# Half strips of the convolution's taps through two buffers, their read-back on the queue of the weights, and three small reorderings at the joints of a four-layer trunk

## The chip, the core and the metric

The kernel runs on one core of a Trainium2 chip. A core has five engines with queues of their own: PE (matrix products; PEld in the profile is its weight load), DVE and ACT (elementwise work), POOL (elementwise work and, here, issuing of some transfers) and SP (which here only issues transfers). Each engine works through its own instructions in the order in which they stand, and waits where another engine or a transfer has not delivered yet. The metric is the device time of one execution in microseconds, the median of the runs; lower is better.

## What is computed

A trunk of four layers over 256 frames of width 1024. Layers 0 and 3 mix the frames by retention, layer 1 by a Conformer convolution, layer 2 by stick-breaking attention, and each layer ends with an MLP with a squared ReLU. The parts of the reference that matter here:

```python
for i in range(DEPTH):                       # DEPTH = 4, kinds 0, 1, 2, 0
    h = rms_norm(x, norm_mix[i])
    m = (retention_mixer, conformer_conv_mixer, stick_breaking_mixer)[i % 3](h, ...)
    x = x + m
    x = x + squared_relu_mlp(rms_norm(x, norm_ffn[i]), ffn_w1[i], ffn_w2[i])   # width 4096
return rms_norm(x, final_norm)

def rms_norm(x, w):
    return x * lax.rsqrt(jnp.mean(x * x, axis=-1, keepdims=True) + EPS) * w

def conformer_conv_mixer(xn, pw1_w, pw1_b, dw_w, dw_b, ln_w, ln_b, pw2_w, pw2_b):
    h = xn @ pw1_w + pw1_b
    a, gate = jnp.split(h, 2, axis=-1)
    h = a * jax.nn.sigmoid(gate)
    h = lax.conv_general_dilated(h, dw_w[:, None, :], (1,), [(30, 0)], ..., feature_group_count=1024) + dw_b
    return jax.nn.silu(layer_norm(h, ln_w, ln_b)) @ pw2_w + pw2_b
```

All weights and the output are float32, and every matrix product is made of three products of rounded parts (high x high, high x low, low x high).

## The kernel before

**Weights.** The weights of all layers are one stream of units of 128x1024 numbers, in the order of a table (PLAN). Two units are one chunk of 1 MB, which SP fetches into a tile `raw` (L348, three buffers). `unit_hi` casts a unit to its high part `wh` on ACT (L360), `unit_lo` takes the rest `wl` on DVE (L367); the pool holds five such pairs. PE then multiplies: `mm_w` (L571 low, L575 high) in the first product of the MLP, `triple` (L687) in its second product, `mm_b` (L555 to L557) in the first product of the convolution. A cast is issued where the program fetches the unit, and stands in ACT's queue at that place.

**Norms.** The sum of squares of x, which the norm ahead of each mixer and MLP needs, is collected by `norm_sq`: a square on ACT (L485) for each of the four tiles of x, and an addition (L490) on POOL or on DVE. `norm_r` turns the sum into a factor through PE (L435) and DVE; `bcast` (L442, L448) spreads a factor over the partitions through PE and ACT into the tile `rb`. The products of a mixer are started on x without the factor; it is multiplied in later. At the joint of two layers `middle` leaves the last part of x to be finished inside the first product of the next mixer, and leaves the last two squares to `norm_late`, which the mixer calls.

In the MLP of a retention layer, ACT's relu (L633) and square (L635) take the output of the first product, after ACT (L599) and DVE (L600) have put its halves together. ACT's buffers for that come from the pool `t2` (tiles `t`), of ten.

**Strips.** Six of the convolution's eight groups of channels are done on PE as products with small diagonal matrices. Those matrices, 18 strips of 128x512, are made in layer 0 by `make_strips`: for each of the 36 halves POOL multiplies a pattern by the taps into a tile `st` (L881), and then POOL issues a transfer of `st` to a strip in the chip's main memory (L885). `st` has one buffer. At the start of the convolution POOL issues 18 transfers that read the strips back into tiles of the pool `big` (L1112, 256 KB each, 36 buffers).

```python
o = self.bc.tile([P, S], F32, name=self.nm("st"), tag="lnb", bufs=1)
nc.gpsimd.tensor_mul(...)                              # L881
nc.gpsimd.dma_start(d[:, e * S : (e + 1) * S], o)      # L885
```

**MLP's second product.** `down` walks over the 16 blocks of rows, first those in MIXED (some by Strassen's scheme from sums of raw weights, L383 to L391 on DVE and ACT), then REST, first the left 512 columns, then the right. The places at which `middle` scales a finished part (L761 on ACT), turns it (L774 on PE) and adds it to x (L781 on DVE) are set by `hook`.

**Order.** PE and DVE keep the order of the program where the code says so (`keep_in_program_order`, `manual_schedule`); elsewhere a scheduler places an instruction, and `issue_after(ins)` forbids it to stand ahead of `ins`.

Of the kernel before, what the change touches and what calls it, by code (L numbers as in the profile page):

```python
# [8 lines left out]
F32 = mybir.dt.float32  # L9
# [6 lines left out]
P = 128  # L16
D = 1024
S = 256
# [224 lines left out]
class Trunk:  # L243
    def __init__(self, ctx, tc, xT, w, prm, cst, fin, gn, out):
        self.tc, self.nc = tc, tc.nc
        self.w_d, self.out_d, self.x_d, self.fin_d, self.gn_d = w, out, xT, fin, gn
        pool = lambda name, bufs, **k: ctx.enter_context(tc.tile_pool(name=name, bufs=bufs, **k))
        self.cp = pool("cp", 1)
        self.raw = pool("raw", 3)
        self.wp = pool("wp", 5)  # L250
        self.zp = pool("zp", 1)
        self.big = pool("big", 36)
        self.t2 = pool("t2", 10)
        self.colp = pool("colp", 3)
        self.bc = pool("bc", 2)
        self.prp = pool("prp", 3)
        self.dram = pool("dram", 2, space=bass.MemoryType.DRAM)
        self.acc_p = pool("acc", 4, space=bass.MemoryType.PSUM)
        self.mis_p = pool("mis", 4, space=bass.MemoryType.PSUM)
        self.n = 0  # L260
        self.un = 0
        self.rest = self.end = None
        self.sums = []
        nc = self.nc
        head = self.cp.tile([P, NP0 + 512], F32, name="head", tag="head")
        self.prm0 = head[:, :NP0]
        self.x = [head[:, NP0:]]
        self.prm = self.cp.tile([P, NPCOL - NP0], F32, name="prm", tag="prm")
        self.cst = self.cp.tile([P, NCCOL], F32, name="cst", tag="cst")
        self.first = [self.raw.tile([P, RAWW], F32, name=f"raw{n}", tag="raw") for n in range(3)]  # L270
        self.ones = self.tmp().bitcast(mybir.dt.bfloat16)[:, :512]
        nc.gpsimd.memset(self.ones, 1.0)
        self.warm(11)

        def weights(n, a, b, queue=nc.sync):
# [60 lines left out]
    def unit_hi(self, key):  # L336
        nc = self.nc
        assert PLAN[self.un] == key, (PLAN[self.un], key)
        o = self.un % UPC
        if o == 0:  # L340
            n = self.un // UPC
            if n < len(self.first):
                self.rawt = self.first[n]
            else:
                self.rawt = self.raw.tile([P, RAWW], F32, name=self.nm("raw"), tag="raw")
                h = 1024 if n < 4 else UPC * 1024
                for a in range(0, UPC * 1024, h):
                    nc.sync.dma_start(self.rawt[:, a : a + h], self.w_d[n][:, a : a + h])  # L348
            i = self.un // UPC - DST
            if 0 <= i < RH:  # L350
                n = CCOL["D"] + i * 384
                self.tc.keep_in_program_order(nc.sync.dma_start(self.cst[:, n : n + 384], self.cst_d[:, n : n + 384]))
        o = self.un % UPC
        src = self.rawt[:, o * 1024 : (o + 1) * 1024]
        hi = self.wp.tile([P, 1024], F32R, name=self.nm("wh"), tag="wh")
        lo = self.wp.tile([P, 1024], F32R, name=self.nm("wl"), tag="wl")
        n = 512 if self.un < 2 * UPC else 1024
        cuts = [slice(i, i + n) for i in range(0, 1024, n)]
        for s in cuts:
            nc.scalar.copy(hi[:, s], src[:, s])  # L360
        self.un += 1
        return hi, lo, src, cuts
# [119 lines left out]
    def norm_sq(self, p, engine=None):  # L482
        nc = self.nc
        q = self.tmp()
        nc.scalar.activation(out=q, in_=self.x[p], func=AF.Square)  # L485
        if self.sq is None:
            self.sq = q
        else:
            a = self.tmp()
            (engine or nc.gpsimd).tensor_add(a, self.sq, q)  # L490
            self.sq = a
# [16 lines left out]


    def norm_late(self):  # L510
        if self.sums:
            with self.tc.issue_after(self.z_ins):
                self.norm_sq(self.sums.pop(0), self.nc.vector)

# [167 lines left out]
    def down(self, i, h, fast, begin, hook):  # L682
# [49 lines left out]
        nc.vector.tensor_add(uq, u, e5)  # L732
        nc.vector.tensor_add(C[1, 1], C[1, 1], uq)

        for c in range(2):
            w, late = {}, REST[-2] if c else REST[-1] + 1
            steps = [(kb, kk, t) for kb in REST if kb < late for kk in range(2) for t in range(2)]
            steps += [(kb, kk, t) for t in range(2) for kb in REST if kb >= late for kk in range(2)]
            for kb, kk, t in steps:
                if kb not in w:  # L740
                    w[kb] = plain(kb, c)
                if c:
                    hook(C, (kb, kk, t))
# [125 lines left out]
    def make_strips(self):  # L869
# [6 lines left out]
        for i in range(len(PET)):  # L876
            for v in vs:
                d = self.dram.tile([P, 512], F32, name=self.nm("strip"), tag=f"strip{len(self.strips)}", bufs=1)
                for e in range(2):
                    o = self.bc.tile([P, S], F32, name=self.nm("st"), tag="lnb", bufs=1)  # L880
                    nc.gpsimd.tensor_mul(  # L881
                        v3(o, 8, 32), self.c("id32", 32).unsqueeze(1).to_broadcast([P, 8, 32]),
                        v[:, i * 16 + e * 8 : i * 16 + e * 8 + 8].unsqueeze(2).to_broadcast([P, 8, 32]),
# [5 lines left out]
    def retention(self, j, nxt):  # L889
# [6 lines left out]
        for h in range(RH):  # L896
            for isk in range(2):
# [4 lines left out]
                else:  # L902
                    with self.tc.issue_after(self.z_ins) if j and not h and isk else nullcontext():
                        args = "ret_w_in", j, isk * D + h * DK, self.zs
                        ps = self.pair_w(*args, keep=h == isk == 0) if j else self.pair_b(*args)
                    for _ in range(2):
                        self.norm_late()
                sq = self.tmp()
                nc.scalar.activation(out=sq, in_=ps, func=AF.Square)
                g = self.tmp()  # L910
# [189 lines left out]
    def conv(self, j, nxt):  # L1100
# [3 lines left out]
        rb = None  # L1104


        strip, h4, hs4 = {}, {}, {}
        for i, d in enumerate(PET):
            strip[d] = []
            for f in range(3):  # L1110
                o = self.bigt()
                nc.gpsimd.dma_start(o, self.strips[3 * i + f])  # L1112
                strip[d].append(o)


        def spread(d0, step):
            t = self.raw.tile([P, RAWW], F32, name=self.nm("raw"), tag="raw")
# [88 lines left out]
        def taps_0(a, b):  # L1206
            for x in range(a, b):
                tap_pool(0, x, r1[0], x == CW0)

        with self.tc.manual_schedule(engines={mybir.EngineType.PE, mybir.EngineType.DVE}):  # L1210
            for n in range(2):
                fetch(n)
            for n in range(16):
                p, part = divmod(n, 4)
                if n == 1:
                    self.norm_late()
                    with self.tc.issue_after(self.z_ins):
                        fetch(2)
                    self.norm_late()
                    with self.tc.issue_after(self.z_ins):  # L1220
                        fetch(3)
                if part == 0:
                    pg, pa = self.acc(), self.acc()
# [7 lines left out]
                with self.joint():  # L1231
                    self.mm_b(
                        (pg, pa)[part // 2], w.pop(n), self.zs, part % 2 * 4, part % 2 == 0, part % 2 == 1,
                        (lambda kk: self.norm_r(False) if kk == 1 else None) if n == 2 else None,
                    )
                if n in (1, 2):
                    fetch(n + 3)
                if n == 2:
                    rb = self.bcast(self.r, "rb")
                    sg = gate_in(0, pg)  # L1240
                if n == 3:
                    fetch(6)
                if part == 1 and p:
                    sg = gate_in(p, pg)
                if part == 3 and p < 3:
# [6 lines left out]
        def taps_pe(d, f, gs=range(NG // 2)):  # L1252
# [6 lines left out]
            for g, j in ((g, j) for g in gs for j in range(4)):  # L1259
                if f == 0:  # L1260
                    x = hs4[d][:, j * SW + g : j * SW + g + P]
                else:
                    o = j * HW + 2 * g + f
                    x = h4[d][:, o : o + 2 * P - 1 : 2]
                nc.tensor.matmul(  # L1265
                    pb[d, f][32 * j : 32 * j + 32], strip[d][f][:, (g * 4 + j) * 32 : (g * 4 + j + 1) * 32], x,
                    start=g == 0, stop=g == NG // 2 - 1, **kw,
                )

# [249 lines left out]
    def stick(self, j, nxt):  # L1519
# [8 lines left out]
        ready = {}  # L1528

        def weight(n):  # L1530
            while len(ready) <= min(n + (SB_AHEAD if n else 1), len(keys) - 1):
                ready[len(ready)] = self.unit(keys[len(ready)])
            return ready[n]

# [213 lines left out]
```

## Time and profile before

| | |
|---|---|
| median of three runs | 1350.38 us (1349.49, 1350.38, 1355.21) |
| profiled execution | 1359.19 us |
| its span, from the first to the last instruction of the profile | 1357.4 us |
| mean granted clock of PE | 0.991 |
| PE busy | 1327.4 us (98%) |
| DVE, ACT, POOL busy | 1060.2, 860.6, 165.4 us |

Section 2 of the page cuts the span into 40 slices of 33.9 us and gives the busy share of each engine and PE's granted clock in tenths. In a timeline a row is the start, the duration, the engine, the line and what the instruction writes and reads; in brackets stands how long its engine had been idle just before and what ended that. A row with x4 is four instructions in a row. In a table by windows each row is a stretch of time, with its length, the busy time of PE, PEld, DVE, ACT and POOL (number of instructions behind each), the granted clock, the share of the transfer engines' time and the GB/s that they moved.

### The profile page before, as it was taken

The page shows a single profiled execution, that of the slowest core. Times are in us where ns is not written, and L with a number is a line of the kernel's source. Part 1 is how long each engine was busy: PE and PEld are TensorE (multiplying, and loading weights), DVE is VectorE, ACT ScalarE, POOL GpSimd, SP SyncE. Part 2 cuts the span into 40 slices and gives each one's busy share as a digit, 9 for nine tenths or more (in the row PEclk, how much of TensorE's full clock was granted, in tenths as well). Part 3 has the DMA queues.
Part 4 walks back from the last instruction along what each step waited for, and adds up shares of the span by engine and source line. Part 5 has one row for each costly group of instructions (what it writes and reads, how often), then busy time and mean ns, then how long its engine had stood idle before and what let it go on. Part 6 is the DMA issues. An engine that isn't in the chain of part 4 may idle for free.

```text
span 1357.4 us, 20252 instructions
## 1 busy us (share of the span) xinstructions
PE 1327.4 (98%) x7703; PEld 1139.4 (84%) x7703; DVE 1060.2 (78%) x1805; ACT 860.6 (63%) x1407; POOL 165.4 (12%) x187
## 2 busy tenths in 40 slices
PE   9999997899999999999999999999999999999998
PEld 8988886788789988888888898888888888888886
DVE  7978864779778678789768778798798776798985
ACT  7555553786557467875558858866576554667663
POOL 3532223000205601000000010000030000100000
PEclk9999998899999999999999999999999999999999
DMA  8556564455855555546643345555564454555552
GB/s 310 207 209 216 207 217 151 159 182 184 301 186 158 154 185 191 186 151 217 217 155 124 125 182 193 186 185 191 181 215 172 177 197 170 187 187 188 199 186 93
DMA packets 44897, 253.95 MB, mean 187 GB/s; under 512 B 5376, under 2 KB 10112, under 8 KB 17408
## 3 DMA queue, kind: packets, MB, share of 16 engines
q1 hardware_dynamic: 40768, 240.60, 50.4%
q0 software_dynamic: 3168, 9.44, 1.9%
q10 hardware_dynamic: 864, 2.62, 0.6%
q8 instruction: 60, 0.98, 0.3%
q14 instruction: 37, 0.30, 0.1%
HBM read 245.99 MB, written 6.65 MB: 186 GB/s over the span
## 4 chain that ended last, share of the span: by engine, by line
PE 79%; DMA 11%; DVE 4%; POOL 3%; issue 2%; ACT 1%; SPq 0%; ACTq 0%; POOLq 0%
PE acc L575 20%; PE acc L687 18%; PE acc L571 10%; DMA strip<-st 10%; PE acc L1095 4%; PE acc L1097 4%; PE acc L1096 4%; PE mis L687 3%; PE acc L555 3%; PE acc L556 3%; PE acc L557 3%; POOL st L881 2%; DMA raw<-in_w 2%; PE acc L1265 1%; DVE wl L367 1%
## 5 line engine op out<-in xcount | busy, mean ns | idle before, releaser
L367 DVE TENSOR_TENSOR wl<-raw,wh 128x1024 fp32r<-128x1024 f32 (+1 forms) x420 | 513.8, 1235 | 136.1 <-ACT wh L360 134.7
L360 ACT CAST wh<-raw 128x1024 fp32r<-128x1024 f32 (+1 forms) x420 | 433.1, 1041 | 235.2 <-PE acc L687 68.4
L575 PE MATMUL acc<-z,wh 128*128 128x512 f32 x1152 | 405.4, 398 | 0.0
L571 PE MATMUL acc<-z,wl 128*128 128x256 f32 x1152 | 320.5, 283 | 12.5 <-DVE t L600 12.5
L575 PEld LDWEIGHTS acc<-z,wh 128*128 128x128 f32 x1152 | 216.9, 190 | 48.9
L687 PE MATMUL acc<-wh,big 128*128 128x512 f32 x800 | 257.1, 392 | 0.0
L571 PEld LDWEIGHTS acc<-z,wl 128*128 128x128 f32 x1152 | 219.5, 191 | 15.5 <-issue 13.1
L687 PEld LDWEIGHTS acc<-wh,big 128*128 128x128 f32 x800 | 150.9, 189 | 31.1
L687 PE MATMUL acc<-wl,big 128*128 128x512 f32 x400 | 157.0, 392 | 2.6 <-DVE wl L367 2.6
L1095 PE MATMUL acc<-wh,z 128*128 128x512 f32 x352 | 138.6, 394 | 0.0
L1096 PE MATMUL acc<-wl,z 128*128 128x512 f32 x352 | 137.3, 390 | 0.4 <-DVE wl L367 0.4
L1097 PE MATMUL acc<-wh,z 128*128 128x512 f32 x352 | 137.3, 390 | 0.0
L687 PEld LDWEIGHTS acc<-wl,big 128*128 128x128 f32 x400 | 75.6, 189 | 20.2 <-DVE wl L367 4.4
L599 ACT COPY t<-acc 128x256 f32<-128x256 f32 x154 | 53.2, 371 | 58.1 <-PE acc L575 56.2
L1095 PEld LDWEIGHTS acc<-wh,z 128*128 128x128 f32 x352 | 66.1, 188 | 15.3 <-issue 2.2
L1097 PEld LDWEIGHTS acc<-wh,z 128*128 128x128 f32 x352 | 66.1, 188 | 14.7 <-issue 0.8
L1096 PEld LDWEIGHTS acc<-wl,z 128*128 128x128 f32 x352 | 66.1, 188 | 14.1 <-DVE wl L367 0.8
L600 DVE TENSOR_TENSOR t<-acc,t 128x256 f32<-128x256 f32 x154 | 59.8, 420 | 18.6 <-ACT t L599 17.3
L390 ACT CAST wh<-t 128x512 fp32r<-128x512 f32 x80 | 47.0, 618 | 38.3 <-PE acc L687 16.4
L555 PE MATMUL acc<-z,wh 128*128 128x256 f32 x224 | 63.7, 284 | 0.0
L556 PE MATMUL acc<-z,wh 128*128 128x256 f32 x224 | 63.4, 283 | 0.0
L557 PE MATMUL acc<-z,wl 128*128 128x256 f32 x224 | 63.4, 283 | 0.0
(301 smaller groups left out, 2067.2 us busy)
## 6 DMA issues: line engine op xcount, KB each, us to landing
raw<-in_w SPq DMA_DIRECT2D x214, 1024.0 KB, 4.9
strip<-st POOLq DMA_DIRECT2D x36, 128.0 KB, 4.0
big<-strip POOLq DMA_DIRECT2D x18, 256.0 KB, 6.0
big<-in_gn SPq DMA_DIRECT2D x16, 256.0 KB, 5.4
raw<-in_w SPq DMA_DIRECT2D x7, 512.0 KB, 7.6
raw<-hd SPq DMA_DIRECT2D x8, 263.0 KB, 4.9
raw<-hd SPq DMA_DIRECT2D x8, 131.5 KB, 3.0
wh<-in_w ACTq DMA_DIRECT2D x2, 512.0 KB, 6.8
```

The source lines that it names most:

```text
L360: nc.scalar.copy(hi[:, s], src[:, s])
L367: self.nc.vector.tensor_sub(lo[:, s], src[:, s], hi[:, s])
L555: nc.tensor.matmul(o, wh[:, kk, cs], ah, start=st, stop=False, **kw)
L556: nc.tensor.matmul(o, wh[:, kk, cs], al, start=False, stop=False, **kw)
L557: nc.tensor.matmul(o, wl[:, kk, cs], ah, start=False, stop=en, **kw)
L571: mm = nc.tensor.matmul(ps[m][:, :S], wl[:, kk, cs], a[:, :S], start=first and kk == 0, stop=False, **kw)
L575: nc.tensor.matmul(ps[m], wh[:, kk, cs], a, start=False, stop=last and kk == 3, **kw)
L600: nc.vector.tensor_add(o[:, s], ps[m][:, :S], o[:, s])
L687: mm = nc.tensor.matmul(o, l, r, start=start and n == 0, stop=stop and n == 2, skip_group_check=True)
L1095: nc.tensor.matmul(ps[t], zh[:, s], wh[:, kk], start=k == 0, stop=False, skip_group_check=True)
L1096: nc.tensor.matmul(ps[t], zh[:, s], wl[:, kk], start=False, stop=False, skip_group_check=True)
L1097: nc.tensor.matmul(ps[t], zl[:, s], wh[:, kk], start=False, stop=k == 7, skip_group_check=True)
```

## The change

It has four parts.

1. The tile `st` of a half strip takes the tags `lnb` and `lnr` in turn, so two halves have a buffer each.
2. The 18 read-backs leave POOL's queue at the start of the convolution. `down` of layer 0 puts them into a list when the blocks in MIXED are done, and `unit_hi` takes two from the list each time it has fetched a chunk, on SP.
3. The last two squares at a joint stand together, ahead of the casts: `norm_late` does both at once, the convolution fetches its third unit at the start and its fourth after the squares, and the attention fetches three units at the start instead of two.
4. In the convolution the broadcast of the norm's factor and the first gate that uses it stand one unit later: in the fourth unit (n == 3) instead of behind the third.

```diff
@@ unit_hi, behind the fetch of a chunk
+            for _ in range(min(2, len(self.later))):
+                self.later.pop(0)()
@@ norm_sq
-        nc.scalar.activation(out=q, in_=self.x[p], func=AF.Square)
+        self.sq_ins = nc.scalar.activation(out=q, in_=self.x[p], func=AF.Square).ins
@@ norm_late
-        if self.sums:
+        while self.sums:
             with self.tc.issue_after(self.z_ins):
                 self.norm_sq(self.sums.pop(0), self.nc.vector)
@@ down, behind the blocks in MIXED, ahead of REST
+        if i == 0:
+            self.strip_t = []
+            def fetch():
+                d = self.strips[len(self.strip_t)]
+                o = self.bigt()
+                self.tc.keep_in_program_order(nc.sync.dma_start(o, d))
+                self.strip_t.append(o)
+            self.later = [fetch] * len(self.strips)
@@ make_strips
-                    o = self.bc.tile([P, S], F32, name=self.nm("st"), tag="lnb", bufs=1)
+                    o = self.bc.tile([P, S], F32, name=self.nm("st"), tag=("lnb", "lnr")[e], bufs=1)
@@ conv
-        strip, h4, hs4 = {}, {}, {}
-        for i, d in enumerate(PET):
-            strip[d] = []
-            for f in range(3):
-                o = self.bigt()
-                nc.gpsimd.dma_start(o, self.strips[3 * i + f])
-                strip[d].append(o)
+        h4, hs4 = {}, {}
...
+        def rsum(kk):
+            if kk == 1:
+                self.norm_r(False)
+        def spread_r(kk):
+            nonlocal rb
+            if kk == 1:
+                rb = self.bcast(self.r, "rb")
+        hooks = {2: rsum, 3: spread_r}
...
-            for n in range(2):
+            for n in range(3):
                 fetch(n)
             for n in range(16):
                 if n == 1:
                     self.norm_late()
-                    with self.tc.issue_after(self.z_ins):
-                        fetch(2)
-                    self.norm_late()
-                    with self.tc.issue_after(self.z_ins):
+                    with self.tc.issue_after(self.sq_ins):
                         fetch(3)
...
-                        (lambda kk: self.norm_r(False) if kk == 1 else None) if n == 2 else None,
+                        hooks.get(n),
...
-                if n == 2:
-                    rb = self.bcast(self.r, "rb")
-                    sg = gate_in(0, pg)
                 if n == 3:
                     fetch(6)
+                    sg = gate_in(0, pg)
@@ stick, weight(n)
-            while len(ready) <= min(n + (SB_AHEAD if n else 1), len(keys) - 1):
+            while len(ready) <= min(n + (SB_AHEAD if n else 2), len(keys) - 1):
```

The rows below are instructions as they stand on an engine: the line, the operation, the tile written and the tiles read, and the size; the number behind a name tells buffers of one name apart, and the lines of the changed kernel are 2 to 13 higher.

POOL at the end of the strips, in layer 0, before. The additions of squares (L490) belong to the norm ahead of the MLP; the first takes the third of the four tiles of x.

```order
L885 DMA strip_1326<-st_1327 128x256
L490 TENSOR_TENSOR t_451_2096<-t_444_2060,t_450_2094 128x512
L881 TENSOR_TENSOR st_1330<-cst,prm 128x256
L885 DMA strip_1326<-st_1330 128x256
L881 TENSOR_TENSOR st_1334<-cst,prm 128x256
L885 DMA strip_1333<-st_1334 128x256
L881 TENSOR_TENSOR st_1337<-cst,prm 128x256
L885 DMA strip_1333<-st_1337 128x256
L490 TENSOR_TENSOR t_478_2264<-t_451_2096,t_477_2262 128x512
L490 TENSOR_TENSOR t_485_2300<-t_478_2264,t_484_2298 128x512
```

The same place after.

```order
L894 TENSOR_TENSOR st_1327<-cst,prm 128x256
L894 TENSOR_TENSOR st_1330<-cst,prm 128x256
L898 DMA strip_1326<-st_1327 128x256
L898 DMA strip_1326<-st_1330 128x256
L894 TENSOR_TENSOR st_1334<-cst,prm 128x256
L894 TENSOR_TENSOR st_1337<-cst,prm 128x256
L898 DMA strip_1333<-st_1334 128x256
L898 DMA strip_1333<-st_1337 128x256
L492 TENSOR_TENSOR t_451_2096<-t_444_2060,t_450_2094 128x512
L492 TENSOR_TENSOR t_478_2264<-t_451_2096,t_477_2262 128x512
L492 TENSOR_TENSOR t_485_2300<-t_478_2264,t_484_2298 128x512
```

Now the products and the transfers of two halves stand in pairs, and all three additions stand behind the last strip, where the first of them stood three halves earlier.

SP from the last chunks of layer 0's MLP to the first of the convolution, before. `raw_3883` and `raw_3947` hold the last four units of the MLP, `raw_4043` the first two of the convolution.

```order
L348 DMA raw_3883<-in_w 128x2048
L348 DMA raw_3947<-in_w 128x2048
L348 DMA raw_4043<-in_w 128x2048
L348 DMA raw_4101<-in_w 128x2048
L348 DMA raw_4139<-in_w 128x2048
```

After: `raw_3959` is the last chunk of the MLP, `raw_4023` the first of the convolution, `raw_4037` its second.

```order
L348 DMA raw_3959<-in_w 128x2048
L743 DMA big_3811<-strip_1214 128x512
L743 DMA big_3813<-strip_1221 128x512
L743 DMA big_3849<-strip_1228 128x512
L743 DMA big_3851<-strip_1235 128x512
L743 DMA big_3893<-strip_1242 128x512
L743 DMA big_3895<-strip_1249 128x512
L743 DMA big_3961<-strip_1256 128x512
L743 DMA big_3963<-strip_1263 128x512
L348 DMA raw_4023<-in_w 128x2048
L743 DMA big_4025<-strip_1270 128x512
L743 DMA big_4027<-strip_1277 128x512
```

Eight read-backs now stand between the last chunk of the MLP and the first of the convolution, the other ten stand in twos behind later chunks, and the 18 rows of L1112 are gone from POOL.

ACT in the first units of the convolution, before. `t_884` and `t_889` are the squares of the third and the fourth tile of x.

```order
L485 ACTIVATE t_884_4097<-x_117 128x512
L360 CAST wh_4103<-raw_4101 128x1024
L360 CAST wh_4111<-raw_4101 128x1024
L360 CAST wh_4141<-raw_4139 128x1024
L360 CAST wh_4188<-raw_4139 128x1024
L485 ACTIVATE t_889_4107<-x_120 128x512
L360 CAST wh_4228<-raw_4226 128x1024
L360 CAST wh_4242<-raw_4226 128x1024
L448 COPY rb_4195<-mis_4192 128x256
L1137 ACTIVATE t_906_4198<-t_905_4197,prm 128x256 x2
L360 CAST wh_4279<-raw_4277 128x1024
```

The same place after.

```order
L487 ACTIVATE t_881_4091<-x_117 128x512
L487 ACTIVATE t_883_4095<-x_120 128x512
L362 CAST wh_4099<-raw_4037 128x1024
L362 CAST wh_4133<-raw_4127 128x1024
L362 CAST wh_4180<-raw_4127 128x1024
L362 CAST wh_4219<-raw_4213 128x1024
L362 CAST wh_4238<-raw_4213 128x1024
L450 COPY rb_4193<-mis_4190 128x256
L362 CAST wh_4279<-raw_4273 128x1024
L1142 ACTIVATE t_907_4224<-t_906_4223,prm 128x256 x2
```

The two squares stand together ahead of the casts; the cast of the third unit (`wh_4043`, not among these rows) has moved up ahead of the scaling of the MLP's last part (L761), and the cast of the ninth unit (`wh_4279`) now stands ahead of the sigmoids (L1137 before).

More of the change, by code (lines that the diff above doesn't have):

```diff
@@ L262, in __init__ @@
         self.rest = self.end = None
-        self.sums = []
+        self.sums, self.later = [], []
         nc = self.nc
@@ L905, in retention @@
                         ps = self.pair_w(*args, keep=h == isk == 0) if j else self.pair_b(*args)
-                    for _ in range(2):
-                        self.norm_late()
+                    self.norm_late()
                 sq = self.tmp()
@@ L1216, in conv @@
                     self.norm_late()
-                    with self.tc.issue_after(self.z_ins):
-                        fetch(2)
-                    self.norm_late()
-                    with self.tc.issue_after(self.z_ins):
+                    with self.tc.issue_after(self.sq_ins):
                         fetch(3)
@@ L1265, in taps_pe @@
                 nc.tensor.matmul(
-                    pb[d, f][32 * j : 32 * j + 32], strip[d][f][:, (g * 4 + j) * 32 : (g * 4 + j + 1) * 32], x,
+                    pb[d, f][32 * j : 32 * j + 32], self.strip_t[3 * PET.index(d) + f][:, (g * 4 + j) * 32 : (g * 4 + j + 1) * 32], x,
                     start=g == 0, stop=g == NG // 2 - 1, **kw,
```

## The prediction

> **What bounds the kernel now.** PE is busy 98% of the span, so only the stretches in which it stands or runs at half clock can shrink. I read the list of waits on PE first. Its rows here are what PE did next, what it waited for, total us, number, longest.
>
> ```profile
> PE acc L571 <- DVE t L600: 12.5, 2, 6.7
> ...
> PE acc L687 <- DVE wl L367: 2.6, 4, 2.1
> PE mis L435 <- DVE t L490: 2.1, 2, 2.0
> ...
> PE mis L442 <- DVE ry L430: 0.6, 1, 0.6
> PE acc L1096 <- DVE wl L367: 0.4, 1, 0.4
> ```
>
> They are four places, and the timelines and windows say what stands behind each. The first row is two stalls in layer 0's MLP. The rows of PE, ACT and POOL around them, the group of the strips' transfers with its landing times and waiter, and the stretch behind each stall beside an equal one later:
>
> ```profile
> 228.19 0.55 PE L571 MATMUL acc<-z,wl 128*128 128x256 f32 x1 [6.68 <-DVE t L600]
> ...
> 242.56 0.55 PE L571 MATMUL acc<-z,wl 128*128 128x256 f32 x1 [5.82 <-DVE t L600]
> ...
> 193.09 0.62 ACT L485 ACTIVATE t<-x 128x512 f32<-128x512 f32 x1
> ...
> 224.59 1.27 POOL L490 TENSOR_TENSOR t<-t,t 128x512 f32<-128x512 f32 x1
> ...
> 225.89 0.63 ACT L633 ACTIVATE t<-t 128x512 f32<-128x512 f32 x1 [8.55 <-POOL t L490]
> ...
> 237.17 2.62 POOL L490 TENSOR_TENSOR t<-t,t 128x512 f32<-128x512 f32 x2
> ...
> 238.48 0.63 ACT L633 ACTIVATE t<-t 128x512 f32<-128x512 f32 x1 [9.82 <-POOL t L490]
> ...
> 235.67 0.61 POOL L881 TENSOR_TENSOR st<-cst,prm 128x256 f32<-128x256 f32 x1 [4.13 <-DMA strip<-st]
> 236.57 0.58 POOL L885 DMA_DIRECT2D strip<-st  x1 [0.30 <-POOL st L881]
> ...
> L881 POOL TENSOR_TENSOR st<-cst,prm x36: 607/611/2949, 58.3 to 235.7; 128x256 f32<-128x256 f32 x36
> ...
>   DMA strip<-st: 111.7, 35
> ...
> DMA to landing us min/median/max: 2.0/4.0/6.3
> ...
> 228.20:234.20 6.00, 6.00 (x19) 5.14 (x20) 1.98 (x4) 0.46 (x1) 2.05 (x2) 0.50 0.55 179
> 242.60:247.90 5.30, 5.30 (x17) 4.52 (x18) 4.82 (x11) 2.63 (x5) 0.00 (x0) 0.50 0.40 136
> 250.00:256.00 6.00, 6.00 (x36) 5.20 (x35) 4.61 (x10) 4.79 (x9) 0.00 (x0) 1.00 0.48 175
> ```
>
> The square of x's third tile is there at 193.71 (193.09 + 0.62), but POOL adds it only at 224.59: in POOL's queue the addition stands behind halves of strips, and each waits with its single buffer for the transfer before (111.7 us in 35 waits). ACT's relu (L633) wants the buffer that the addition frees and waits 8.55 us; L599 and L600 queue behind it, PE's accumulators are not emptied, and PE stands. It happens again at 238.48. Behind each stall PE runs at clock 0.50.
>
> The stall of the second row stands in `down`, where POOL's read-backs share the transfer engines with the weights: the landing of a weights' chunk takes 9.19 us instead of the 4.9 of the page's median, and DVE waits 4.59 us for it.
>
> ```profile
> 352.46 0.50 PE L687 MATMUL acc<-wl,big 128*128 128x512 f32 x1 [2.12 <-DVE wl L367]
> ...
> 339.44 9.19 DMA raw<-in_w
> ...
> raw<-in_w SPq DMA_DIRECT2D x214, 1024.0 KB, 4.9
> big<-strip POOLq DMA_DIRECT2D x18, 256.0 KB, 6.0
> ...
> 348.65 0.69 DVE L383 TENSOR_TENSOR t<-raw 128x512 f32<-128x512 f32 x1 [4.59 <-DMA raw<-in_w]
> ...
> 343.70:347.10 3.40, 3.40 (x17) 2.82 (x16) 0.36 (x1) 1.40 (x2) 1.64 (x3) 1.00 0.99 387
> 353.70:357.10 3.40, 3.40 (x9) 2.64 (x8) 3.39 (x5) 0.53 (x1) 0.00 (x0) 0.50 0.73 247
> ```
>
> The other rows are the joints. At the first, ACT does four casts between the third square and the fourth, and PE's sum of squares waits for the fourth:
>
> ```profile
> 412.41 0.80 PE L435 MATMUL mis<-cst,t 128*128 128x1 f32 x6 [1.97 <-DVE t L490]
> ...
> 406.61 0.61 ACT L485 ACTIVATE t<-x 128x512 f32<-128x512 f32 x1
> 407.13 3.87 ACT L360 CAST wh<-raw 128x1024 fp32r<-128x1024 f32 x4
> 410.91 0.62 ACT L485 ACTIVATE t<-x 128x512 f32<-128x512 f32 x1
> ...
> 411.57 0.69 DVE L490 TENSOR_TENSOR t<-t,t 128x512 f32<-128x512 f32 x1 [2.15 <-ACT t L485]
> ```
>
> **The change part by part.** *A, the strips.* Two halves become one cycle: two products (2 x 0.61), the step to the issue (0.30), the first issue (0.58 before the second starts) and a landing of 4.0: 6.1 us. Eighteen cycles are 110 us, so the chain that started at 58.3 ends near 168. With every landing at the longest, 6.3, a cycle is 8.4 and the end 209. PE does not stand if the first addition is done by 225.86 - 6.68 = 219.2; its inputs are ready at 193.71, so from 193.7 to 210.3 (209 + 1.27) it is in time by both bounds, and so are the next two, which need only their squares. The stalls go whole: 6.68 + 5.82 = 12.50. At clock 0.50 the first window holds 19 products in 6.00 us, where the full clock does 36 (0.167 each): 6.00 - 19 x 0.167 = 2.83 more, in the second 5.30 - 17 x 0.167 = 2.47. Together 17.8. In layer 3, where the same MLP has no strips on POOL, nothing else is late behind it; all of this window is PE's:
>
> ```profile
> 1175.00:1200.00 25.00, 25.00 (x150) 22.13 (x149) 20.03 (x43) 15.70 (x28) 2.98 (x2) 1.00 0.50 171
> ```
>
> *B, the read-back.* The stall of 2.12 goes with POOL's transfers, and the half clock behind it: 17 products against 9 in 3.40 us, so 8 x 0.2 = 1.6. Together 3.7.
>
> By the Trainium skill ("TensorE: Matmul & The Clock Gate", Part 1: The HAM clock gate) the clock halves after an idle window of some 3.4 us. By that rule a gap of 2.12 would cost no clock, and the result below would be 1.6 higher, 1337.2; this trace disagrees, with 0.50 granted from 353.7 to 357.1 behind just that gap.
>
> Eight read-backs now stand on SP between the MLP's last chunk and the convolution's first. What waits there:
>
> ```profile
> 376.66 0.33 SPq L348 DMA_DIRECT2D raw<-in_w  x1
> ...
> 390.95 1.05 ACT L360 CAST wh<-raw 128x1024 fp32r<-128x1024 f32 x1 [1.67 <-PE acc L687]
> 391.91 1.26 ACT L761 ACTIVATE t<-acc,r 128x512 f32<-128x512 f32 x2
> ...
> 393.48 1.03 PE L774 MATMUL mis<-cst,t 128*128 128x128 f32 x8
> ```
>
> From the issue at 376.66 the queue holds 1.05 MB, eight strips of 0.26 and 1.05 MB for the convolution: 4.19 MB. At the 387 GB/s of the full stretch above that is 10.8 us; a chunk's landing of 4.9 is 2.2 longer than its own 2.7 at that rate. So the convolution's first chunk lands at 376.66 + 10.8 + 2.2 = 389.7. The cast of the convolution's first unit stands at 390.95, ahead of the scalings that PE's turn at 393.48 needs (391.91 + 1.26 = 393.17, 0.3 to spare). So 389.7 is in time by 1.2 (1.5 with what is to spare), and I cost the block at nothing; this cover is thin and is the second rival. The lower bound is nothing, since the chunk itself arrives no earlier than needed before. SP's own issues, 0.33 each, are nine in 3 us, inside the 10.8. The later twos stand behind chunks that ACT casts in one row only after 407.
>
> *C, the joints.* The fourth square stands right behind the third: 407.2 instead of 410.91, 3.7 earlier, more than the wait of 1.97 that it ends. The casts move 0.6 later. All rows of the joints in the first list go: 2.1 + 0.6 + 0.4 = 3.1, where the 0.6 (the factor's broadcast, waiting for DVE's ry) goes because the broadcast stands a unit later.
>
> *D, the factor a unit later, and the cast of the ninth unit ahead of the sigmoids.* The first gate comes later by a unit, and the cast's 1.05 us delays the sigmoids, behind which stands the chain of taps on ACT and POOL:
>
> ```profile
> 423.17 28.86 POOL L1186 TENSOR_TENSOR big<-big,pr 128x256 f32<-128x256 f32 x29 [31.84 <-ACT pr L1182]
> 451.99 1.06 POOL L1157 TENSOR_TENSOR t<-raw 128x524 f32<-128x524 f32 x1
> ...
> 456.24 1.09 PE L1265 MATMUL acc<-t,big 128*32 128x128 f32 x32
> ```
>
> POOL is busy in it without a gap from 423.17 to 452.0, and then makes the sums that PE takes from 456.24; two of them at 1.06 leave 2.1 us of slack (456.24 - 452.0 - 2 x 1.06). PE loses 3.1 us of waits ahead of it, the chain only a part. The give-back lies between nothing and 3.1 - 2.1 + 1.05 = 2.1; I take 1.0, the middle.
>
> **The sum.** 17.8 + 3.7 + 3.1 = 24.6, less 1.0, is 23.6 against the profiled execution's 1359.19: 1335.6. That execution is 8.8 above the median of the runs, 1350.38. Which base is right is a choice. The only large thing in the kernel that can differ from run to run is the chain of 36 landings, of 2.0 to 6.3 us: 0.24 us more in each is 8.8 at its end, and PE waits for that end. I take it that the profiled execution had a longer chain than the runs, so the runs lose fewer microseconds to it and end at the same 1335.6 without it, 14.8 below their median.
>
> **The rivals.**
>
> *R1, the first weights of the convolution are late.* If the block on SP moves at the 247 GB/s of the window at 353.7 instead, 4.19 MB take 17.0, and with 2.2 the chunk lands at 395.9, 4.9 behind the cast's old place; less 0.3, PE stands 4.6, and pays 1.6 of half clock as at 353.7: 1335.6 + 6.2 = 1341.8. For it: ten transfers of both kinds share the engines, as in the stretch that stalls now. Against: one queue works here, and the same engines moved 387 GB/s in the full stretch. It decides from 338 GB/s down (4.19 MB in 391.25 - 376.66 - 2.2 = 12.4 us).
>
> The Trainium skill ("DMA: Bandwidth & Descriptors", Queues, rings and completion order) has each transfer engine take a queue's descriptors in ring order, so weights issued behind strips start behind them, as this rival and the estimate both assume; its Specifications give some 358 GB/s for a core's memory, by which the landing is estimated at 390.6, still in time; the measured stretch, at 387, is above that figure.
>
> *R2, the profile is evenly slower.* If the 8.8 lie all over the span, the runs lose the whole 23.6: 1350.38 - 23.6 = 1326.8. For it: nothing in one profile excludes it. Against: the runs themselves differ by 5.7, as a chain of landings would make them.
>
> *R3, two buffers hardly shorten the chain.* If two transfers in flight slow each other to landings above 6.8 us ((217.9 - 58.3)/18 - 2.1, where 217.9 is 219.2 - 1.27), the stalls stay in part: with half of 17.8 left, 1335.6 + 8.9 = 1344.5, within 0.5%. For it: the longest landing, 6.3, is near that already. Against: the median is 4.0, and the transfer engines are busy only 0.40 to 0.55 of the windows there.
>
> *R4, slower than before: SP's queue stands.* SP issues everything in order, so a read-back that waits holds all weights behind it. It decides against the change if the weights come 21.5 us late in sum (1357.1 - 1335.6); with 18 read-backs that is a loss of 1.2 us each. For it: three buffers of weights are all the cover. Against: their tiles of `big` were freed long before (the 18 take their places from blocks done in MIXED), and at 387 GB/s the 4.7 MB of all are 12.2 us, spread over 50 us with the engines half free. It would give 1358 or more.
>
> **How the numbers follow.** A measurement of this kernel tells about 0.5% from no change, 6.75 us: faster is below 1343.6, slower above 1357.1. The forecast, 1335.6 with its own range of 1334.6 (no give-back) to 1339.4 (a give-back of 2.1, and half of A's clock loss of 5.3 kept, 2.7), has 0.60. R1 has 0.14, R2 0.14, R3 0.06, R4 0.04; 0.02 is left for a part of the change that is absent in the result. R1 and R2 set the range: 1326 to 1343. Faster are the forecast, R1 and R2: 0.88; same R3 and the rest, 0.08; slower R4, 0.04.
>
> **What the profile after would show.** A: no L571 wait for L600 near 228 and 243, the last strip issued before 210, no ACT wait for POOL's L490, clock 1.0 there. B: no wait of PE near 352, weights landing near 4.9 us, no POOL transfer. R1: ACT idle for `raw` ahead of the cast that stands at 390.95 now and near 369 then, and PE waiting at L774 or at the first L555. C: the wait before L435 gone. D: PE waiting for POOL's sums at L1265. Wrong would be: a chain that ends after 219, weights that land in over 12 us behind the strips, or runs that keep the profile's 8.8.

## The result and the profile after

The changed kernel takes 1329.35 us (median of 1328.73, 1329.23, 1329.47 and 1330.34); the kernel before takes 1349.97 beside it. The ratio is 0.9839, with a 95% interval of 0.9814 to 0.9864: faster by 1.6%. The profiled execution took 1329.23 us with a span of 1327.5, so here the profile stands on the median, while the one of before stood 9.2 above it.

The list of PE's waits of the changed kernel, in the columns of before (next instruction and what it waited for, total us, number, longest):

```profile
PE acc L1275 <- issue: 1.4, 3, 0.9
PE mis L300 <- POOL t L272: 1.3, 1, 1.3
PE acc L619 <- DVE z L477: 0.7, 1, 0.7
PE acc L689 <- DVE wl L369: 0.5, 3, 0.2
```

Of the waits in layer 0's MLP, of the read-back's 2.1 and of those at the joints no row is left; L300 and L619 are the start of the kernel.

The strips: the group of POOL's products, its waits for their transfers, the landing times, and the end of POOL's work on them in the timeline. Then the windows in which PE passes the places of the three half-clock windows of before.

```profile
L894 POOL TENSOR_TENSOR st<-cst,prm x36: 608/656/2547, 60.5 to 171.8; 128x256 f32<-128x256 f32 x36
...
  DMA strip<-st: 54.8, 19
...
DMA to landing us min/median/max: 2.0/4.0/6.3
...
172.32 1.11 POOL L898 DMA_DIRECT2D strip<-st  x2
193.10 1.30 POOL L492 TENSOR_TENSOR t<-t,t 128x512 f32<-128x512 f32 x1 [19.66 <-ACT t L487]
220.50:226.50 6.00, 6.00 (x37) 5.30 (x36) 4.50 (x9) 4.38 (x8) 0.00 (x0) 1.00 0.67 247
226.50:231.80 5.30, 5.30 (x32) 4.68 (x31) 4.79 (x9) 4.46 (x8) 0.00 (x0) 1.00 0.57 199
329.00:333.50 4.50, 4.50 (x22) 3.72 (x21) 4.07 (x6) 2.98 (x6) 0.00 (x0) 1.00 0.71 231
```

The least, middle and longest landing are those of before, but two run side by side: POOL waits 54.8 us for them where it waited 111.7, and is done at 173.4 instead of 237. The first addition then waits for ACT's square, not ACT for POOL. In 6.00 us PE does 37 products where 19 fitted.

The block on SP: SP's timeline, the landing of the chunk issued at 358.61 (the convolution's first), ACT's cast of it and PE's turn.

```profile
352.91 0.33 SPq L348 DMA_DIRECT2D raw<-in_w  x1
353.35 4.80 SPq L743 DMA_DIRECT2D big<-strip  x8
358.61 0.33 SPq L348 DMA_DIRECT2D raw<-in_w  x1
...
DMA to landing us min/median/max: 7.1/7.1/7.1
...
367.20 1.05 ACT L362 CAST wh<-raw 128x1024 fp32r<-128x1024 f32 x1 [1.67 <-PE acc L689]
...
369.73 1.03 PE L787 MATMUL mis<-cst,t 128*128 128x128 f32 x8
```

The chunk lands at 358.61 + 7.1 = 365.7 and the cast at 367.20 waits for PE, not for it: 1.5 us to spare.

The first joint in ACT's and PE's timelines, and the convolution's taps on POOL with the first sum that PE takes:

```profile
382.86 1.14 ACT L487 ACTIVATE t<-x 128x512 f32<-128x512 f32 x2
383.90 3.88 ACT L362 CAST wh<-raw 128x1024 fp32r<-128x1024 f32 x4
386.53 0.39 PE L437 MATMUL mis<-cst,t 128*128 128x1 f32 x3
396.92 28.87 POOL L1191 TENSOR_TENSOR big<-big,pr 128x256 f32<-128x256 f32 x29 [29.34 <-ACT pr L1187]
425.74 1.07 POOL L1162 TENSOR_TENSOR t<-raw 128x524 f32<-128x524 f32 x1
429.46 1.07 PE L1275 MATMUL acc<-t,big 128*32 128x128 f32 x32
```

PE's sum of squares at 386.53 has no wait in front of it. The taps start 26.25 us earlier than before, PE's first use of their sums 26.78 (456.24 - 429.46): the chain lost 0.5 us against PE and its slack bore it.

PE runs the same 7703 products in both kernels, in the same order but for the four of the broadcast, which stand six products later, and for some neighbours in the taps. So the start of each can be subtracted from the start of the one in its place before. This is where the 30 us between the two profiled executions arose:

| stretch (times of before) | gained by its end, us | in it |
|---|---|---|
| start of the kernel | 0.3 | 0.3 |
| 221 to 248, the two stalls and half clocks | 18.4 | 18.2 |
| 248 to 345 | 19.7 | 1.2 |
| 345 to 358, the read-back | 23.7 | 4.0 |
| 405 to 418, first joint | 26.8 | 3.1 |
| 470 to 485, taps on PE (L1275) | 28.5 | 1.7 |
| 689 to 696, second joint | 29.7 | 1.1 |
| rest | 30.0 | 0.3 |

### The profile page after: what moved, and what is told of

Read it like the earlier page. It is cut to its first block, busy times and chain, and to the rows that moved or that the text cites. A ratio compares the mean times of both kernels' runs of the same rounds, so it can differ in the third digit from the quotient of the medians.

```text
span 1327.5 us, 20237 instructions
## 1 busy us (share of the span) xinstructions
PE 1316.6 (99%) x7703; PEld 1133.6 (85%) x7703; DVE 1063.9 (80%) x1805; ACT 860.1 (65%) x1407; POOL 154.1 (12%) x169
## 4 chain that ended last, share of the span: by engine, by line
PE 96%; DVE 2%; ACT 1%; DMA 0%; issue 0%
PE acc L577 22%; PE acc L689 19%; PE acc L573 11%; PE acc L1107 6%; PE acc L1109 6%; PE acc L1108 6%; PE mis L689 3%; PE acc L557 3%; PE acc L558 3%; PE acc L559 3%; PE mis L577 2%; PE acc L1275 1%; PE mis L573 1%; PE acc L1408 1%; DVE wl L393 1%; DVE t L385 1%
## 5 line engine op out<-in xcount | busy, mean ns | idle before, releaser
L577 PE MATMUL acc<-z,wh 128*128 128x512 f32 x1152 | 399.4, 393 | 0.0
L573 PE MATMUL acc<-z,wl 128*128 128x256 f32 x1152 | 317.6, 280 | 0.0
L577 PEld LDWEIGHTS acc<-z,wh 128*128 128x128 f32 x1152 | 214.2, 187 | 47.1
L492 POOL TENSOR_TENSOR t<-t,t 128x512 f32<-128x512 f32 x15 | 24.2, 1612 | 339.1 <-ACT t L487 308.7
```

Of the source, the lines that this page charges most:

```text
L573: mm = nc.tensor.matmul(ps[m][:, :S], wl[:, kk, cs], a[:, :S], start=first and kk == 0, stop=False, **kw)
L577: nc.tensor.matmul(ps[m], wh[:, kk, cs], a, start=False, stop=last and kk == 3, **kw)
```

## The experiments

**The strips' second buffer alone**, in the kernel before:

```diff
-  o = self.bc.tile([P, S], ..., tag="lnb", bufs=1)
+  o = self.bc.tile([P, S], ..., tag=("lnb", "lnr")[e], bufs=1)
```

> The kernel before with only the half strips' second buffer. Theory (each part removes its own stall, and POOL's queue order carries the strips' chain to PE): the last strip is issued near 173 us, the two waits of PE at 228 and 243 and the half clock behind them go, the stalls at the read-back and at the joints stay: 1329.4 + 4.3 (read-back) + 4 to 5 (joints) = about 1338.5. Rival (transfers in flight side by side slow each other as soon as the read-back is not moved too, or the gain needs the other parts): a chain that ends after 210, PE's wait at L571 still there, 1345 or more.

Measured 1336.65 (1334.64 to 1336.72), ratio 0.9891 (0.9868 to 0.9915). The last strip is issued at 173.1, and of PE's waits only those of the other parts are left:

```profile
PE mis L435 <- DVE t L490: 2.1, 2, 2.0
PE acc L687 <- DVE wl L367: 2.1, 4, 1.6
```

So the buffer alone brings most of the gain and needs no other part: 18.2 us between 221 and 248, as in the whole change. The time is 1.9 under the expected 1338.5 mainly because the read-back cost 1.9 here, not 4.3 (below).

**One buffer in the changed kernel**, the same edit the other way.

> The changed kernel with one buffer for the half strips again. Theory: both waits of PE in layer 0's MLP come back, as large as the chain of 36 landings is long in that execution; with the 9.2 by which the profiled execution before stood above the median as the size of that variation, 1329.4 + 10 to 19 = 1339 to 1349. Rival (the profiled execution before was evenly slower, and the strips' chain is worth little): under 1336.

Measured 1345.15 (1343.23 to 1350.34, ten runs). In the profiled execution, 1350.34, PE's list and the group of the strips' issues read:

```profile
PE acc L573 <- DVE t L602: 16.7, 2, 9.9
...
L898 POOL DMA_DIRECT2D strip<-st x36: 580/580/709, 65.3 to 239.8; - x36
```

Both stalls are back. The rival's bound of 1336 is out of reach. The spread of 7 us in ten runs, against 1.6 in four of the changed kernel, came back with the chain too.

**The kernel before, once more**, for a second profile.

> The kernel before once more, for a second profile. Theory (the profiled execution before was 9.2 above the median because its chain of strips ended late): the chain's end, PE's two waits and the time move together; with a time near 1350, the last strip is issued some 9 us before 237 and the two waits and their half clock are some 9 us shorter in sum. Rival (that execution was evenly slower): at 1350 the chain ends near 237 and the waits are as large.

It took 1350.86. PE's list, then POOL's timeline at the end of the strips:

```profile
PE acc L571 <- DVE t L600: 8.6, 1, 8.6
...
217.11 1.30 POOL L490 TENSOR_TENSOR t<-t,t 128x512 f32<-128x512 f32 x1
...
230.46 0.58 POOL L885 DMA_DIRECT2D strip<-st  x1 [0.30 <-POOL st L881]
231.06 2.62 POOL L490 TENSOR_TENSOR t<-t,t 128x512 f32<-128x512 f32 x2
```

The chain ended 6.1 us earlier than in the first profile (230.46 against 236.57), one of the two stalls is gone, and the stretch of 221 to 248 costs 11.7 instead of 18.2: 6.5 less. The first profile was not evenly slower. The expectation had put some 9 us on the chain; of the 8.3 between the two profiles another 3.4 are PE's waits in the convolution's taps, which this execution does not have (last section), and 1.6 went the other way in smaller places. The stall that is gone is the first: the first addition is done at 218.41 (217.11 + 1.30), and ACT waits only 0.64 for it. Three executions with one buffer lie close to one line: last issue at 230.5, 236.6, 239.8, and 11.7, 18.2, 20.2 lost; the loss is the time of the last issue less about 219 (218.4 to 219.6).

**The additions of squares on DVE** in the kernel before, the strips left as slow as they are:

```diff
-            self.norm_pair(p, *nxt)
+            self.norm_pair(p, *nxt, False)
+            self.norm_sq(p, nc.vector if nxt[1] == 0 else None)
...
-                    sums = self.norm_sums()
+                    sums = self.norm_sums(nc.gpsimd if i else nc.vector)
```

> The kernel before with the three additions of squares, and the last sum, ahead of layer 0's MLP on DVE instead of POOL. The strips' chain stays as it is, one buffer, to about 237 us. Theory (the stalls come from POOL's queue, in which the additions stand behind the strips, and not from the transfers or the buffers of the strips): ACT no longer waits at L633, PE's two waits at L571 and the half clock go, as with two buffers: about 1338.5. Rival (the strips' transfers or POOL's products slow ACT and DVE themselves): the waits stay, 1345 or more.

Measured 1335.55 (1334.73 to 1337.32), ratio 0.9876 (0.9839 to 0.9914). The last strip is issued late, as before, but ACT's relu does not wait:

```profile
230.22 0.58 POOL L885 DMA_DIRECT2D strip<-st  x1 [0.30 <-DVE big L410]
...
217.28 0.64 ACT L633 ACTIVATE t<-t 128x512 f32<-128x512 f32 x1
```

That settles the cause of the large term: the queue order on POOL, not the transfers or the products of the strips. Both edits that free the additions from the slow chain, the second buffer and this one, gain 18.2 us between 221 and 248. This kernel lost nothing at the read-back either, which still ran on POOL (309.5 to 346.7), which more than makes the 3 us under the expected 1338.5. Its two chunks of weights issued from 315 to 325 land in 6.0 and 8.3 us, where with the second buffer alone they took 8.4 and 10.3; what makes them faster was not tested.

**The read-back on POOL again**, in the changed kernel:

```diff
-                self.tc.keep_in_program_order(nc.sync.dma_start(o, d))
+                nc.gpsimd.dma_start(o, d)
...
+        for _ in self.strips:          # at the convolution's start
+            self.fetch_strip()
```

> The changed kernel with the 18 read-backs on POOL's queue at the convolution's start again. Theory: a weights' chunk lands in over 8 us near 330 to 340 us, DVE waits for it, PE stands some 2 us and runs at half clock for 3.4 us: 1329.4 + 3.7 to 4.3 = 1333 to 1334. Rival (the read-back on POOL hurts only because POOL's queue was late with the strips): no wait, 1329.4.

Measured 1333.97 (1329.35 to 1334.56). PE's list, the landing of the two chunks issued from 316 to 325, and DVE's wait for one of them:

```profile
PE acc L689 <- DVE wl L369: 2.0, 4, 1.5
...
DMA to landing us min/median/max: 8.3/9.2/10.2
...
328.48 1.29 DVE L385 TENSOR_TENSOR t<-raw 128x512 f32<-128x512 f32 x2 [3.96 <-DMA raw<-in_w]
```

The mechanism is the same: weights late, a wait on DVE, a wait on PE. But PE lost only 1.8 us there, without half clock; with the buffer alone, 1.9, without half clock too. It was 4.0 and 4.4 in the two profiles of the kernel before. The rest of what this profile lost, 3.2 us, arose in the convolution's taps and is not the read-back's (below), so the median, inside the expected range, is there by luck and overstates the part. One of the four runs took 1329.35, no longer than the changed kernel: the times alone do not tell a part of 1.8 from the waits in the taps.

**The squares behind the casts again**, in the changed kernel: `norm_late` does one square a call, the convolution fetches its third and fourth unit behind the squares, and the attention two units at the start.

> The changed kernel with the joints' squares behind the casts again, the broadcast still a unit later. Theory: PE waits some 2 us for the sum of squares at the joint to the convolution and 0.6 to 1.1 at the joint to the attention: 1329.4 + 2.6 to 3.3 = 1332 to 1332.7. Rival (with the broadcast a unit later the sum is no longer needed early, so the squares' place is free): 1329.4 to 1330.0 and no wait of PE at L437.

Measured 1335.38 (1333.16 to 1335.77). PE's list, and a window behind the first joint:

```profile
PE mis L437 <- DVE t L492: 2.1, 2, 2.0
...
391.30:394.70 3.40, 3.40 (x18) 3.40 (x18) 3.09 (x13) 1.04 (x1) 0.00 (x0) 0.50 0.76 292
```

The wait of 2.0 is back, and this time half clock followed it, 1.6 us, which the same wait had not brought in the first profile of before. At the first joint PE lost 3.7, at the second 1.1: 4.8, more than expected.

**The broadcast behind the third unit again**, in the changed kernel:

```diff
-        hooks = {2: rsum, 3: spread_r}
+        hooks = {2: rsum}
...
+                if n == 2:
+                    rb = self.bcast(self.r, "rb")
+                    sg = gate_in(0, pg)
```

> The changed kernel with the factor's broadcast and the first gate behind the third unit of the convolution again. Theory: PE's wait at the broadcast for DVE's ry comes back, 0.6 us, and the taps' chain on ACT and POOL starts about a unit earlier, which gains nothing since it has slack: 1329.4 + 0.6 = 1330.0. Rival (the chain of taps is late in the changed kernel and the part costs what it saves): 1329.4 or lower, with the waits at L1275 shorter.

Measured 1329.71 (1329.25 to 1331.70). Product by product PE loses nothing to the changed kernel between 221 and 440 us: no wait at the broadcast. The part is worth nothing where the squares are early. I then undid both:

> The changed kernel with the joints' squares behind the casts and the broadcast behind the third unit, both as in the kernel before; the strips' two buffers and the read-back on SP stay. Theory (the broadcast a unit later is worth something only where the squares are late): PE waits 2.0 for the sum of squares and another 0.6 for ry, so the stretch around the first joint loses 0.6 more than with the squares alone undone, 2.7 to 4.3 there in all, and about 1.1 at the second: 1333.5 to 1336. Rival (the broadcast's place is worth nothing either way): no wait at the broadcast, and the same time as with the squares alone undone.

Measured 1334.15 (1333.59 to 1335.67), against 1335.38 with the squares alone undone. Again no wait at the broadcast. PE ran at half clock there, which may have given DVE the time, so whether the part would save its 0.6 us at full clock stays open; in these runs it saved at most 0.3.

**All 18 read-backs ahead of the convolution's first chunk:**

```diff
-            for _ in range(min(2, len(self.later))):
+            for _ in range(len(self.later)):
```

> The changed kernel with all 18 read-backs ahead of the convolution's first chunk of weights, where 8 stand. Theory (SP works through its queue in order, at the full rate of the transfer engines): the chunk lands at 352.9 + 6.82 MB / 387 GB/s + 2.2 = 372.7, 5.2 behind the time at which it is cast now (367.2, with 0.3 to spare); PE stands some 5 us near 370 and runs at half clock behind it for 3.4 us: 1329.4 + 6.8 = 1336. Rival (the read-backs and the weights share the engines evenly, so a later chunk is not held back by all of them): no wait, 1329.4.

Measured 1331.55 (1329.20 to 1334.01), and no loss against the changed kernel up to 440 us. SP's timeline, and ACT's:

```profile
353.53 11.82 SPq L743 DMA_DIRECT2D big<-strip  x18
365.65 12.28 SPq L348 DMA_DIRECT2D raw<-in_w  x4
...
367.62 1.29 ACT L774 ACTIVATE t<-acc,r 128x512 f32<-128x512 f32 x2 [1.90 <-DVE acc L759]
...
374.14 1.99 ACT L362 CAST wh<-raw 128x1024 fp32r<-128x1024 f32 x2
```

The queue did as the theory had it: the 18 held SP for 11.82 us, and the chunk behind them landed 7.0 after its issue, at 372.7, the time expected to the tenth. The stall did not come, because the scheduler put the cast behind the scalings (L774) that PE's turn needs: 374.14 against 367.62. My expectation had kept the old order on ACT. What a late cast ahead of the scalings costs was therefore not seen.

**The changed kernel once more:**

> The changed kernel once more. Theory: 1329.4 with a spread under 2 us, no wait of PE in layer 0's MLP, at the read-back or at the joints; what varies is PE's wait at L1275 in the convolution, between some 0.5 and 4 us (with half clock behind the longer ones), as in the profiles of the other kernels, and each such wait ends 2.2 to 2.9 us after the start of a transfer of instructions. Rival (those waits come from the tiles of the convolution that pass through main memory): the wait ends with such a landing.

Measured 1330.89 (1330.02 to 1332.49), ratio 0.9824 (0.9790 to 0.9858); the spread of 2.5 is over the 2 expected. The profiled execution, 1332.49, differs from the first of this kernel at one place. PE's timeline, and of the transfer queues in 450.30 to 450.45 the row of instructions:

```profile
444.20 0.55 PE L1275 MATMUL acc<-raw,big 128*32 128x128 f32 x10 [0.96 <-issue]
452.59 0.42 PE L1275 MATMUL acc<-raw,big 128*32 128x128 f32 x2 [2.23 <-issue]
...
q8 instruction: 1, 0.02, 40.3%
```

PE waited 2.23 at 452.59, and ran at half clock from 452.49 for 3.4 us. A transfer of 16 KB on the queue named "instruction" had started at 450.39, 2.2 us before PE went on. The convolution's tiles had all landed by 441 (the last was issued at 435.5, none took over 4.6 there in this or the first profile), so the rival falls.

## Why the prediction was right, and where its sum was off

The forecast was 1335.6 with 1326 to 1343; 1329.35 lies inside, 6.3 lower than forecast. It lies outside the forecast's own narrower range, 1334.6 to 1339.4, and nearer to R2's 1326.8, whose mechanism did not occur: that the wide range holds it is partly luck. The profile's fall was 30.0, the sum 23.6. Of what is missing, 2.8 belong to the parts (A 0.4, B 0.3, C 1.1, D 1.0); 3.5 arose where the prediction names nothing (1.2 behind the stalls, 1.7 in the taps on PE, 0.6 at the start and in the rest), and no part of the change is shown to have caused them.

- **A** was right in cause and size: 18.2 in its stretch against 17.8; POOL was done at 173.4 where the cycle of 6.1 us gave 168. The threshold, the first addition done by 219.2, holds too: done at 218.41 (second profile of before) it costs no stall, done at 225.86 (first profile) and 229.26 (one buffer in the changed kernel) it goes with stalls of 6.68 and 9.88. Not in the sum were the 1.2 us from 248 to 345. From 249 to 310 PE's products start 176.7 ns apart on average in both profiles of the kernel before, and 173.3 in all other runs. That the changed kernel with one buffer has 173.3 too shows that the chain is not the cause; which one it is stays open.
- **B** was 4.0 against 3.7 in this pair of executions. The experiments show that it is not a fixed price: 1.8 to 1.9, without half clock, with the second buffer, and nothing with the additions on DVE. Together with the second buffer the part is worth half of its term.
- **C** was mis-sized: 4.2 (3.1 and 1.1) against 3.1, since the second joint gave 1.1 where the list showed 0.4; and where the squares are late again the loss reaches 4.8, since half clock may follow.
- **D**, the give-back of 1.0, failed: nothing was given back, and PE has no wait for POOL's sums. The taps on PE were 1.7 faster instead, which is chance: PE's waits with "issue" there sum to 2.8 in the first profile of before, nothing in the second, and 1.4 and 3.2 in the two of the changed kernel. The cost of one cast ahead of the sigmoids was met by the slack that the prediction itself had counted; taking the middle of its range was wrong, with the slack (2.1) above the chain's loss (0.5). The 0.6 put under C for the broadcast came with the earlier squares, not with the later broadcast.
- **The base.** The choice that the profile of before had a longer chain than the runs was right for the greater part (the second profile: 6.1 earlier, 6.5 less lost), and R2's even slowness is refuted by the same two profiles. But the prediction laid the whole 8.8 on the chain; the waits in the taps, 3.4 in that pair, differ from execution to execution as well. The runs after lie where the profile after does, so the miss of 6.3 against the median is that of the sum against the profile. Against the median the gain was 20.6, not 30, because the median run before is 9.2 faster than the profile; by the second profile most of that is the shorter chain.
- **R1** did not come: landing at 365.7, where the prediction's 389.7 less the 23.7 gained until then is 366.0, and 1.5 to spare. **R3** did not: no landing over 6.3 in this profile with two in flight, where 6.8 was its bound. **R4** did not: even 18 read-backs in a row held SP for only 11.82 us.

## What to carry to other kernels

A helper engine that is busy 12% of the time can still set the end: look at what stands in its queue behind a chain of single-buffered transfers, and compare the time at which the first victim there gets done with the time at which it is needed. A second buffer that overlaps two landings, or moving the victim to another queue, bought the same here. Where one profile stands well above the median, take a second one before deciding which stall varies: here two profiles of the kernel before told the chain's length (6.5 us) apart from the waits in the taps (3.4).

## What the runs showed of the hardware

- **Half clock comes in whole windows and after short waits.** Inside the span its stretches lasted 3.41, 6.83 or 10.24 us, one to three times 3.413. Within each of the twelve profiles all edges of the granted clock lie whole multiples of 3.413 us apart (223.96, 234.20, 241.03, 247.85, 353.67 and 357.08 in the first of before), while the first edge stands elsewhere in each, between 4.1 and 6.5 us. Waits of PE of 1.81, 1.87, 2.12, 2.23, 2.48 and 2.50 us were followed by one; the wait of 1.96 to 1.97 at the first joint brought one in four profiles and none in the two of the kernel before; 1.88 brought none once, nor did 1.49, 1.60 or less. The Trainium skill ("TensorE: Matmul & The Clock Gate", Part 1: The HAM clock gate) has windows of 3413 ns that run freely, and has the clock halve after an idle window of that length. The edges agree with the first; for the second, 1.8 to 2.5 us of wait were enough here. Where a wait lies in its window fits the mixed results at the first joint: the window that holds the end of the wait had PE idle for 0.98 to 1.47 us in the four profiles with half clock, and for 0.92 and 0.71 in the two without. Idle time alone is not the whole measure, since elsewhere a window with 1.62 us brought half clock and one with 1.88 did not. A stall of 2 us is thus worth 2.0 or 3.6 us.
- **PE's waits in the taps come with transfers of instructions.** In ten of the twelve profiles PE waits in the convolution's taps, in products of 32 columns that take some 0.03 us each in a row, with "issue" as the cause. Of the 20 such waits of 0.24 us or more, 19 ended 2.2 to 2.8 us after the start of a 16 KB transfer on the queue "instruction", and one, of 0.30, 3.4 after it; in the two profiles without such waits those transfers came some 4 us apart, where those ahead of the 19 waits came 5.2 to 8.6 after the one before. The waits sum to between nothing and 3.4 us, and with the half clock behind the longer ones they make most of the few us by which the profiles of the changed kernel still differ. That the transfer is what PE waits for is read from this coincidence; no run changed it.
